# Joining projections side by side: matmuls of 512 columns in a two-layer decoder trunk

## The chip, the cores and the metric

One core of one Trainium2 chip. The metric is the time of one execution in device microseconds (us), as the median of several runs of the same kernel.

## The reference

A decoder trunk of two layers on 256 tokens and a model width of 1024, all in float32. Layer A is differential attention with a bias by distance, layer B is attention over a shared compressed latent; each is followed by a gated feed-forward with a short causal convolution and by a gated embedding. Only the projections in front of the two attentions matter here:

```python
# layer A: 8 heads, two maps of 64 each; x is (256, 1024), w_qkv is (1024, 3072)
qkv = rms_norm(x, attn_norm) @ w_qkv
q = rms_norm(qkv[:, :1024].reshape(256, 8, 2, 64), q_gain)        # a norm over each 64
k = rms_norm(qkv[:, 1024:2048].reshape(256, 8, 2, 64), k_gain)
v = qkv[:, 2048:].reshape(256, 8, 128)
# layer B: 16 heads; c_kv is (256, 256), c_q is (256, 512)
kv = (c_kv @ w_ukv).reshape(256, 16, 256)
k_nope, v = rms_norm(kv[..., :128], k_gain), kv[..., 128:]        # a norm over each 128
qq = (c_q @ w_uq).reshape(256, 16, 192)
q_nope = rms_norm(qq[..., :128], qn_gain)                          # a norm over each 128
q_pe = rotary(rms_norm(qq[..., 128:], qp_gain), pos)               # a norm over each 64
```

## The kernel before

Every float32 operand is held as two numbers of the type fp32r, a high part and a low part, and each product is made of three matmuls that add up in PSUM: high by high, high by low, low by high (`mm3`, L197). PE is TensorE, DVE VectorE, ACT ScalarE, POOL GpSimd, SP the engine that issues most DMAs.

**Weights.** The host cuts all weights into units of 128 x 1024 values (512 KB), in the order of their use (`_layout`, L1230). `load_unit` (L250) fetches the next unit into a ring of buffers and splits it: ACT casts the high part (`wh`, L246), and DVE or POOL subtracts it to get the low part (`wl`, L247). A share, 0.5 in layer A and 0.3 in most of layer B, says how many of these subtractions POOL takes. The ring has five buffers for fetched units and four pairs for split ones. SP issues the fetches in the order of the program, and a fetch whose buffer is not free holds all that follow it.

**Projections of layer A** (`proj_a`, L497). Four calls, each for two heads, and in each three blocks (`s` = 0, 1, 2): q, k and v, of 256 columns each. A block has eight k-tiles of 128 and two tiles of 128 tokens. The activations are the stationary operand of a matmul, the weights the moving one. `block` (L376) runs all k-tiles for the first token tile and then for the second one; both write halves of the same PSUM bank, which holds 512 values a partition. Two units, of four k-tiles each, feed a block. The first block of all (`first_block`, L675) takes its units as they come from DMA, in pieces of 256 KB with pieces of the activations between them; it splits both k by k on ACT and DVE (`get_first`, L663), 256 columns at a time, and uses a bank for each token tile.

**Norms** (`norm_block`, L337). ACT squares (L347 with a sum for blocks of 128, L350 for blocks of 64), DVE sums (L351) and adds epsilon (L353, L355), POOL takes the power -1/2 (L280), DVE multiplies out of PSUM (L361). A list of banks is squared and multiplied bank by bank. In layer A the epsilon carries the mean square of the token (`xs["eps"]`); it needs the statistics of the input, which `first_stats` (L688) loads and sums. Then `to_T` (L366) transposes by PE (L193) and splits the result (ACT L208, DVE L209); this is put off by `later`, for `LAG` = 6 us of the planner's own count of PE time.

**Order.** The builder's planner simulates the engines and sets from that, in advance, the order of instructions on each engine; on the chip each runs in that order. In the attention stages `weave` (L161) mixes two streams in the program: attention, and a filler (the projections still to come, the output projection). `bias_prep` (L399) makes the masks of the bias on DVE and 16 matmuls that sum them (L430); it is called from `proj_a` of the second head pair, and the planner puts its work into gaps from about 13 us on. The copies of its result (`bias_loads`, L451) are issued by SP after the fetches of units 10 to 12.

**Projections of layer B.** The order of the filler is `B_ORDER` (L63). An item ("kv", p) makes key and value for two heads: one unit with two k-tiles, each 256 key columns and 256 value columns; `kv_b` (L1090) runs a block for the key, its norm, and a block for the value into another bank. An item ("pe", c) makes the rotary parts of the queries of four heads (`pe_b`, L1110), an item ("qn", p) the other query parts of two heads (`qn_b`, L1129): a unit, a block and a norm each. Banks come from `bankF` (L1080): the first twelve by a list of the tags A, B and C, then always from tag A, which has three banks. The compressed query is ready after `cq_post`; an attention head needs its key, value and query, and its rotary part.

## Time and profile before

| | |
|---|---|
| three runs, median (lowest to highest) | 778.34 us (777.44 to 778.69) |
| the profiled execution | 777.55 us |
| its span, first to last instruction | 775.8 us |
| PE, DVE, ACT, POOL busy | 753.3, 570.8, 485.1, 272.7 us |
| mean granted clock of PE | 0.995 |
| read from memory | 125.75 MB |

The profile shows one execution. "Busy" is the time in which an engine has at least one instruction under way; matmuls overlap, so the mean duration of one is longer than the distance from one start to the next. A wait is idle time of an engine just before an instruction, with the one that ended it. The chain of work that ended last is followed back from the last instruction, each time to what released it. Times in rows count from the first instruction.

### The profile page before, as it was taken

To read this page: it belongs to the slowest core of one execution; us is meant where nothing else is said; L and a number is where in the kernel's file an instruction comes from. 1 tells how busy PE (TensorE), PEld (TensorE's weight loads), DVE (VectorE), ACT (ScalarE), POOL (GpSimd) and SP (SyncE) were. 2 spreads that over 40 slices of the span, in tenths; PEclk is the share of its full clock that TensorE was granted. 3 is DMA by queue.
4 is the path that set the end of the run, shared out by engine and by line. 5 is a ranking of instruction groups with operands and counts; after the bars stand their busy time and mean duration, and the time that the engine had idled before them with its cause. 6 is when DMAs were issued, how large, how long until landed. Compare 5 with 4: busy or idle time off the path is not lost.

```text
span 775.8 us, 16482 instructions
## 1 busy us (share of the span) xinstructions
PE 753.3 (97%) x6396; PEld 740.0 (95%) x6396; DVE 570.8 (74%) x1141; ACT 485.1 (63%) x1044; POOL 272.7 (35%) x187
## 2 busy tenths in 40 slices
PE   7999999999999999999898999999999999999996
PEld 6999989999999999999798999999999999999996
DVE  6677888568997796546788887876688778875545
ACT  6537876676566665447766876564676666655442
POOL 2655464232332511115616555221342332201231
PEclk9999999999999999999999999999999999999999
DMA  8994444256665576655354133344465566565531
GB/s 293 278 234 160 134 150 136 82 187 181 195 190 177 181 230 216 190 165 176 117 164 166 43 98 112 108 136 135 138 191 189 170 185 195 187 185 174 187 108 55
DMA packets 37519, 127.97 MB, mean 165 GB/s; under 512 B 4672, under 2 KB 6208, under 8 KB 37440
## 3 DMA queue, kind: packets, MB, share of 16 engines
q1 hardware_dynamic: 36432, 126.29, 52.5%
q8 instruction: 50, 0.82, 0.4%
q10 hardware_dynamic: 1008, 0.63, 0.3%
q14 instruction: 29, 0.24, 0.1%
HBM read 125.75 MB, written 1.15 MB: 164 GB/s over the span
## 4 chain that ended last, share of the span: by engine, by line
PE 82%; DVE 8%; ACT 4%; POOL 3%; issue 2%; DMA 1%; SPq 0%; POOLq 0%; ACTq 0%; DVEq 0%
PE pa L199 17%; PE pa L200 17%; PE pa L201 17%; PE pc L201 8%; PE pc L200 8%; PE pc L199 8%; DVE wl L247 2%; POOL wl L247 1%; DVE og L209 1%; ACT wh L246 1%; PE pt L193 1%; POOL s L280 1%; PE pb L482 1%; PE pb L549 1%; PE pc L193 1%
## 5 line engine op out<-in xcount | busy, mean ns | idle before, releaser
L246 ACT CAST wh<-st 128x1024 fp32r<-128x1024 f32 x221 | 230.8, 1049 | 166.5 <-issue 61.2
L247 DVE TENSOR_TENSOR wl<-st,wh 128x1024 fp32r<-128x1024 f32 x160 | 204.6, 1280 | 99.4 <-ACT wh L246 95.8
L247 POOL TENSOR_TENSOR wl<-st,wh 128x1024 fp32r<-128x1024 f32 x61 | 149.6, 2452 | 224.9 <-ACT wh L246 200.2
L201 PE MATMUL pa<-hgH,wl 128*128 128x256 f32 x496 | 140.7, 284 | 0.4 <-POOL wl L247 0.4
L199 PE MATMUL pa<-hgH,wh 128*128 128x256 f32 x496 | 140.4, 283 | 0.0
L200 PE MATMUL pa<-hgL,wh 128*128 128x256 f32 x496 | 140.3, 283 | 0.0
L200 PE MATMUL pa<-og,wh 128*128 128x256 f32 x352 | 99.8, 284 | 0.9 <-DVE og L209 0.9
L199 PE MATMUL pa<-og,wh 128*128 128x256 f32 x352 | 100.2, 288 | 0.1
L201 PE MATMUL pa<-og,wl 128*128 128x256 f32 x352 | 100.1, 285 | 0.0
L199 PE MATMUL pa<-wh,hgH 128*128 128x256 f32 x328 | 93.5, 289 | 4.8 <-DVE d L361 1.7
L304 POOL TENSOR_TENSOR ssq<-ssq,d 128x256 f32<-128x256 f32 x35 | 37.1, 1059 | 172.8 <-ACT d L303 172.4
L201 PE MATMUL pc<-hgH,wl 128*128 128x256 f32 x336 | 95.6, 285 | 1.0 <-DVE wl L247 1.0
L201 PEld LDWEIGHTS pa<-hgH,wl 128*128 128x128 f32 x496 | 95.2, 192 | 0.6 <-POOL wl L247 0.6
L200 PE MATMUL pc<-hgL,wh 128*128 128x256 f32 x336 | 95.1, 283 | 0.1
L199 PEld LDWEIGHTS pa<-hgH,wh 128*128 128x128 f32 x496 | 95.1, 192 | 0.1
L200 PEld LDWEIGHTS pa<-hgL,wh 128*128 128x128 f32 x496 | 95.1, 192 | 0.1
L199 PE MATMUL pc<-hgH,wh 128*128 128x256 f32 x336 | 95.0, 284 | 0.0
L200 PE MATMUL pa<-wl,hgH 128*128 128x256 f32 x328 | 93.4, 286 | 1.5 <-DVE wl L247 0.8
L201 PE MATMUL pa<-wh,hgL 128*128 128x256 f32 x328 | 93.1, 286 | 0.1
L200 PEld LDWEIGHTS pa<-og,wh 128*128 128x128 f32 x352 | 67.7, 192 | 1.1 <-DVE og L209 1.1
L199 PEld LDWEIGHTS pa<-wh,hgH 128*128 128x128 f32 x328 | 62.0, 191 | 6.9 <-DVE d L361 1.9
L199 PEld LDWEIGHTS pa<-og,wh 128*128 128x128 f32 x352 | 67.2, 192 | 0.8 <-ACT og L208 0.3
(304 smaller groups left out, 1913.6 us busy)
## 6 DMA issues: line engine op xcount, KB each, us to landing
st<-in_wall SPq DMA_DIRECT2D x225, 512.0 KB, 3.6
oh<-s SPq DMA_DIRECT2D x24, 128.0 KB, 6.6
hT<-in_x SPq DMA_DIRECT2D x4, 256.0 KB, 5.1
st<-in_wall SPq DMA_DIRECT2D x4, 256.0 KB, 5.3
st<-in_xn SPq DMA_DIRECT2D x2, 512.0 KB, 7.2
d<-in_p SPq DMA_DIRECT2D x2, 256.0 KB, 4.7
out_h<-hT SPq DMA_DIRECT2D x4, 128.0 KB, 1.9
out_h<-hT ACTq DMA_DIRECT2D x4, 128.0 KB, 1.9
```

Source lines behind the costliest of these rows:

```text
L193: lastmm[0] = T.transpose(o, i, ident).ins
L199: T.matmul(ps, lhsT=aH, rhs=bH, start=start, stop=False)
L200: T.matmul(ps, lhsT=aH, rhs=bL, start=False, stop=False)
L201: lastmm[0] = T.matmul(ps, lhsT=aL, rhs=bH, start=False, stop=stop).ins
L209: V.scalar_tensor_tensor(lo, src, scale, f(hi), ALU.mult, ALU.subtract)
L246: A.copy(hi, st)
L247: eng.tensor_sub(lo, st, f(hi))
L280: G.tensor_tensor(dst, src, neghalf[:, :n], ALU.pow)
L304: sqlast[0] = G.tensor_add(sq, sq, t).ins
L482: T.matmul(ps[:, i * 32:(i + 1) * 32], lhsT=lh, rhs=tb[z], start=z == 0, stop=z == 2)
L549: T.matmul(pss[e][:, a:b], lhsT=x[rows, j, t * P:(t + 1) * P], rhs=y[rows, j, :b - a], start=start, stop=stop)
```

## The change

Layer A: the host lays out q and k of a head pair side by side, two k-tiles of 512 columns to a unit, four units for both; v stays as it was. `proj_a` runs, for each token tile, all eight k-tiles with 512 moving columns into one bank (`wide`), and norms that bank (256 columns of q, 256 of k) as soon as it is there. The transposes of q and of k are both scheduled after the second tile's norm and take their sources from two tiles. The first block does q and k of the first pair in this way, from four units that come in halves. Layer B: `kv_b` does key and value in one pass of 512 columns, with a bank for each token tile; `pq_b` does four heads' rotary parts and two heads' other query parts in one pass; the remaining items ("qn", p) with odd p stay as they were. `B_ORDER` follows from that.

```diff
@@ -61,10 +61,10 @@
 def _b_order():
-    order = [("kv", 0), ("kv", 1), ("pe", 0), ("qn", 0), ("qn", 1), ("kv", 2), ("qn", 2), ("pe", 1)]
-    for p in range(3, 8):
-        order += [("kv", p)] + ([("pe", p // 2)] if p % 2 == 0 else []) + [("qn", p)]
-    order.insert(order.index(("qn", 6)) + 1, ("wo", (0, 4)))
+    order = [("kv", 0), ("kv", 1), ("pq", 0), ("qn", 1), ("kv", 2), ("pq", 1), ("kv", 3), ("qn", 3)]
+    for p in range(4, 8):
+        order += [("kv", p), ("qn", p) if p % 2 else ("pq", p // 2)]
+    order.insert(order.index(("pq", 3)) + 1, ("wo", (0, 4)))
     return order + [("wo", (4, 4)), ("wo", (8, 4))]
...
@@ -251,11 +250,10 @@
     first = []
-    for i in range(2):
-        pieces = fetch(2)
-        for k in (4 * i, 4 * i + 2):
-            nc.sync.dma_start(hT[:, k:k + 2], xT[:, k:k + 2])
-            st = next(pieces)
+    for i in range(4):
+        nc.sync.dma_start(hT[:, 2 * i:2 * i + 2], xT[:, 2 * i:2 * i + 2])
+        for st in fetch(2):
+            pass
         first.append(st)
...
@@ -384,6 +386,14 @@
                     k += 1
+
+    def wide(t, units, lH, lL, ps):
+
+        for i, u in enumerate(units):
+            for j in range(2):
+                k, c = 2 * i + j, slice(j * 512, (j + 1) * 512)
+                mm3(ps, lH[:, k, t * P:(t + 1) * P], lL[:, k, t * P:(t + 1) * P], u[0][:, c], u[1][:, c], k == 0,
+                    k == 2 * len(units) - 1)
...
@@ -495,41 +505,43 @@
     def proj_a(p):
-        todo = []
-
-        def post(s, ps):
-            dH, dL = qk(), qk()
-            if s < 2:
-                src = norm_block(ps, 4, 64, xs["eps"])
-                if p == 1:
-                    bst["after"] = bst.get("after", []) + nbv
-
-                def fin():
-                    to_T(src, dH, dL, gq[:, 0:1] if s == 0 else col(C_AK))
-                    QA[p]["qk"[s]] = dH, dL
-                later(LAG, fin)
-            else:
-                for t in range(NT):
-                    split(dH[:, t], dL[:, t], ps[:, t * S:(t + 1) * S], xs["r"][:, t:t + 1])
-                QA[p]["v"] = dH, dL
-
-        for s in range(3):
-            if p == 0 and s == 0:
-                ps = first_block()
-            else:
+        srcs = []
+
+        def norm_qk(t, ps):
+            srcs.append(norm_block(ps, 4, 64, xs["eps"][:, t]))
+            if p == 1:
+                bst["after"] = bst.get("after", []) + nbv
+
+        def fin(s, dH, dL):
+            to_T([x[:, s * S:(s + 1) * S] for x in srcs], dH, dL, gq[:, 0:1] if s == 0 else col(C_AK))
+            QA[p]["qk"[s]] = dH, dL
+
+        if p == 0:
+            pss = first_block()
+            yield 1
+            epsx()
+            first_stats()
+            for t in range(NT):
+                norm_qk(t, pss[t])
+        else:
+            us = [load_unit() for i in range(4)]
+            for t in range(NT):
                 ps = bankA()
-                us = [(load_unit(), 4) for i in range(2)]
-                block(8, us, S, 0, S, hgH, hgL, ps)
-            yield 1
-            todo.append((s, ps))
-            if p == 0 and s == 0:
-                epsx()
-            elif p == 0 and s == 1:
-                first_stats()
-            elif p == 1 and s == 0:
-                bias_prep()
-            while "r" in xs and todo:
-                post(*todo.pop(0))
+                wide(t, us, hgH, hgL, ps)
+                yield 1
+                if p == 1 and t == 0:
+                    bias_prep()
+                norm_qk(t, ps)
+        for s in range(2):
+            later(LAG, lambda s=s, pr=(qk(), qk()): fin(s, *pr))
+        us = [load_unit() for i in range(2)]
+        ps = bankA()
+        block(8, [(u, 4) for u in us], S, 0, S, hgH, hgL, ps)
+        yield 1
+        dH, dL = qk(), qk()
+        for t in range(NT):
+            split(dH[:, t], dL[:, t], ps[:, t * S:(t + 1) * S], xs["r"][:, t:t + 1])
+        QA[p]["v"] = dH, dL
...
@@ -662,10 +674,10 @@
-        for i in range(2):
+        for i in range(4):
             u = ring_pair()
-            for j in range(4):
-                k, q = 4 * i + j, slice(j * S, (j + 1) * S)
+            for j in range(2):
+                k, q = 2 * i + j, slice(j * 512, (j + 1) * 512)
                 A.activation(hgH[:, k], hT[:, k], AF.Copy, scale=col(C_ATTN[0] + k))
...
@@ -676,8 +688,8 @@
             for t in range(NT):
-                mm3(ps[t][:, :S], hgH[:, k, t * P:(t + 1) * P], hgL[:, k, t * P:(t + 1) * P],
-                    u[0][:, j * S:(j + 1) * S], u[1][:, j * S:(j + 1) * S], k == 0, k == NK - 1)
+                mm3(ps[t], hgH[:, k, t * P:(t + 1) * P], hgL[:, k, t * P:(t + 1) * P],
+                    u[0][:, j * 512:(j + 1) * 512], u[1][:, j * 512:(j + 1) * 512], k == 0, k == NK - 1)
         return ps
...
@@ -1091,15 +1102,14 @@
         u = load_unit()
-        ps = bankF()
-        block(2, [(u, 2)], 512, 0, S, ckH, ckL, ps)
-        yield 1.3
-        src = norm_block(ps, 2, P, EPS)
-        ps = bankF()
-        block(2, [(u, 2)], 512, S, S, ckH, ckL, ps)
-        yield 1.3
+        pss = [bankF() for t in range(NT)]
+        for t in range(NT):
+            wide(t, [u], ckH, ckL, pss[t])
+        yield 2.6
+        src = norm_block(pss, 2, P, EPS)
         kH, kL, vH, vL = qk(), qk(), qk(), qk()
-        split(vH.rearrange("p t x -> p (t x)"), vL.rearrange("p t x -> p (t x)"), ps)
+        for t in range(NT):
+            split(vH[:, t], vL[:, t], pss[t][:, S:])
...
@@ -1107,14 +1117,25 @@
-    def pe_b(c):
+    def q_fin(p, src):
+        qH, qL = qk(), qk()
+
+        def fin():
+            to_T(src, qH, qL, gq[:, 1:2])
+            QB[p]["q"] = qH, qL
+        later(LAG, fin)
+
+    def pq_b(c):
         while not cq_ready:
             yield None
-        u = load_unit()
-        ps = bankF()
-        block(4, [(u, 4)], S, 0, S, cqH, cqL, ps)
-        yield 2.6
-        qn = norm_block(ps, 4, 64, EPS)
+        us = [load_unit() for i in range(2)]
+        pss = []
+        for t in range(NT):
+            pss.append(bankF())
+            wide(t, us, cqH, cqL, pss[t])
+            yield 2.6
+        qn = norm_block(pss, 4, 64, EPS)
+        q_fin(2 * c, norm_block([x[:, S:] for x in pss], 2, P, EPS))
         qr = d_tile()
...
@@ -1266,8 +1281,9 @@
     for p in range(4):
-        for s in range(3):
-            natural(wqkv[:, s * 1024 + p * 256:s * 1024 + (p + 1) * 256], 4)
+        q, k, v = (wqkv[:, s * 1024 + p * 256:s * 1024 + (p + 1) * 256] for s in range(3))
+        natural(np.concatenate([q, k], axis=1), 2)
+        natural(v, 4)
     wo = f("a_w_o")[0]
...
@@ -1284,17 +1300,17 @@
-    def qpe(c):
-        natural(uq[:, 4 * c:4 * c + 4, P:].reshape(512, 256), 4)
-
     def qn(p):
-        natural(uq[:, 2 * p:2 * p + 2, :P].reshape(512, 256), 4)
+        return uq[:, 2 * p:2 * p + 2, :P].reshape(512, 256)
+
+    def pq(c):
+        natural(np.concatenate([uq[:, 4 * c:4 * c + 4, P:].reshape(512, 256), qn(2 * c)], axis=1), 2)
     for nm, a in B_ORDER:
         if nm == "wo":
             blocks(stationary(wo, range(a[0], a[0] + a[1])))
         else:
-            {"kv": kv, "pe": qpe, "qn": qn}[nm](a)
+            {"kv": kv, "pq": pq, "qn": lambda p: natural(qn(p), 4)}[nm](a)
     blocks(stationary(wo, range(12, 16)))
     ffn(1)
     wall = np.stack(units)

...
```

## Rows read from the trace of the kernel before

**Rows 1.** The page: busy time by engine, chain by engine.
```profile
PE 753.3 (97%) x6396; PEld 740.0 (95%) x6396; DVE 570.8 (74%) x1141; ACT 485.1 (63%) x1044; POOL 272.7 (35%) x187
...
PE 82%; DVE 8%; ACT 4%; POOL 3%; issue 2%; DMA 1%; SPq 0%; POOLq 0%; ACTq 0%; DVEq 0%
```

**Rows 2.** Timeline of PE: start, us, instruction, count, idle before, releaser.
```profile
5.74 0.50 PE L199 MATMUL pa<-wh,hgH 128*128 128x256 f32 x2 [0.97 <-ACT wh L671]
...
12.81 0.28 PE L201 MATMUL pa<-wh,hgL 128*128 128x256 f32 x1
...
14.77 0.83 PE L430 MATMUL pb<-ge,identb 128*128 128x384 bf16 x4
16.41 0.39 PE L200 MATMUL pa<-wl,hgH 128*128 128x256 f32 x1 [0.81 <-DVE wl L247]
...
19.33 0.38 PE L200 MATMUL pa<-wl,hgH 128*128 128x256 f32 x1 [0.57 <-POOL wl L247]
```

**Rows 3.** Windows: stretch, length, busy (count) by engine, clock, DMA share, GB/s.
```profile
4.00:13.00 9.00, 7.84 (x54) 6.72 (x54) 7.51 (x26) 6.22 (x17) 0.00 (x0) 1.00 1.00 368
26.00:50.00 24.00, 24.00 (x247) 23.99 (x245) 16.82 (x26) 10.46 (x15) 13.65 (x7) 1.00 1.03 238
600.00:620.00 20.00, 20.00 (x169) 20.00 (x168) 15.51 (x30) 12.36 (x22) 7.22 (x3) 1.00 0.55 178
```

**Rows 4.** Waits of PE in 395 to 530 us: us in total, times, longest.
```profile
PE pa L199 <- DVE d L361: 1.7, 1, 1.7
PE pa L199 <- DVE qk L206: 1.4, 1, 1.4
```

**Rows 5.** Timeline of PE: first and last of 23 projection matmuls of 256 columns.
```profile
23.11 0.28 PE L201 MATMUL pa<-wh,hgL 128*128 128x256 f32 x1
...
25.75 0.28 PE L199 MATMUL pa<-wh,hgH 128*128 128x256 f32 x1
```

**Rows 6.** Timeline of PE: four starts at 320 columns, 27 at 512.
```profile
381.18 0.31 PE L200 MATMUL pb<-wl,og 128*128 128x320 f32 x1
...
381.62 0.45 PE L201 MATMUL pb<-wh,og 128*128 128x320 f32 x2
...
385.80 0.40 PE L199 MATMUL pc<-wh,og 128*128 128x512 f32 x1
...
391.72 0.39 PE L201 MATMUL pc<-wh,og 128*128 128x512 f32 x1
```

**Rows 7.** Tile st, 0 to 30 us: count, ns min/median/max, starts.
```profile
L671 ACT CAST wh<-st x8: 388/402/407, 5.3 to 10.9; 128x256 fp32r<-128x256 f32 x8
L672 DVE TENSOR_TENSOR wl<-st,wh x8: 418/420/423, 5.8 to 11.7; 128x256 fp32r<-128x256 f32 x8
L246 ACT CAST wh<-st x7: 1040/1047/1058, 13.4 to 29.4; 128x1024 fp32r<-128x1024 f32 x7
L247 DVE TENSOR_TENSOR wl<-st,wh x3: 1220/1221/2053, 15.1 to 24.3; 128x1024 fp32r<-128x1024 f32 x3
L247 POOL TENSOR_TENSOR wl<-st,wh x3: 2405/2495/3766, 15.5 to 26.1; 128x1024 fp32r<-128x1024 f32 x3
```

**Rows 8.** Timeline of ACT: the activations' casts in the first block.
```profile
6.21 0.91 ACT L669 ACTIVATE hgH<-hT,cst 128x256 fp32r<-128x256 f32 x2 [0.21 <-DMA hT<-in_x]
```

**Rows 9.** Timelines of ACT and POOL: sixth unit's cast, first norm's power.
```profile
20.38 1.05 ACT L246 CAST wh<-st 128x1024 fp32r<-128x1024 f32 x1 [1.24 <-DMA st<-in_wall]
...
20.53 2.36 POOL L280 TENSOR_TENSOR s<-s,neghalf 128x8 f32<-128x8 f32 x1
```

**Rows 10.** Groups by shape, 395:530: count, busy us, mean ns, idle.
```profile
L361 DVE TENSOR_TENSOR d<-pa,s 128x512 f32<-128x512 f32 x18 | 12.3, 685 | 3.0 <-POOL s L280 2.9
L206 DVE TENSOR_TENSOR qk<-pa,qk 128x512 fp32r<-128x512 f32 x6 | 4.1, 683 | 0.0
...
L206 DVE TENSOR_TENSOR og<-pc,og 128x256 fp32r<-128x256 f32 x13 | 5.4, 414 | 0.2 <-ACT og L205 0.2
...
L280 POOL TENSOR_TENSOR s<-s,neghalf 128x4 f32<-128x4 f32 x16 | 17.9, 1117 | 34.4 <-DVE s L353 34.3
```

More of the change, by code (lines that the diff above doesn't have):

```diff
@@ L227, in fetch @@
         for j in range(pieces):
+            if j:
+                yield st
             lastfetch[0] = nc.sync.dma_start(st[:, j * n:(j + 1) * n], wall[u, :, j * n:(j + 1) * n]).ins
@@ L230, in fetch @@
                 hooks.pop(u)()
-            if pieces > 1:
-                yield st
-        if pieces == 1:
-            yield st
+        yield st
     def ring_pair(tag="w", bufs=BUF_W):
@@ L346, in norm_block @@
             for i in range(m):
-                A.activation(s2[:, i * P:(i + 1) * P], ps[:, i * P:(i + 1) * P], AF.Square, accum_out=ss[:, i:i + 1])
+                p, o = parts[i * len(parts) // m], (i % (m // len(parts))) * P
+                A.activation(s2[:, i * P:(i + 1) * P], p[:, o:o + P], AF.Square, accum_out=ss[:, i:i + 1])
         else:
@@ L366, in to_T @@
     def to_T(src, dH, dL, gcol, bank=None):
-        nb = src.shape[1] // (NT * P)
+        if not isinstance(src, list):
+            z = src.shape[1] // NT
+            src = [src[:, t * z:(t + 1) * z] for t in range(NT)]
+        nb = src[0].shape[1] // P
         pt = (bank or bankT)()
@@ L371, in to_T @@
             for j in range(nb):
-                i, o = t * nb + j, j * NT + t
-                transpose(pt[:, o * P:(o + 1) * P], src[:, i * P:(i + 1) * P])
+                o = j * NT + t
+                transpose(pt[:, o * P:(o + 1) * P], src[t][:, j * P:(j + 1) * P])
         split(dH.rearrange("p n x -> p (n x)"), dL.rearrange("p n x -> p (n x)"), pt[:, :NT * nb * P], gcol)
@@ L696, in first_stats @@
         rsqrt_(xs["r"], m, NT)
-        ep = cp.tile([P, 8], F32, name="epsx")
-        V.tensor_scalar(ep.rearrange("p (t n) -> p t n", t=NT), m.unsqueeze(2).to_broadcast([P, NT, 4]), EPS,
-                        None, ALU.mult)
+        ep = cp.tile([P, NT, 8], F32, name="epsx")
+        V.tensor_scalar(ep, m.unsqueeze(2).to_broadcast([P, NT, 8]), EPS, None, ALU.mult)
         xs["eps"] = ep
@@ L1135, in qn_b @@
         yield 2.6
-        src = norm_block(ps, 2, P, EPS)
-        qH, qL = qk(), qk()
-        def fin():
-            to_T(src, qH, qL, gq[:, 1:2])
-            QB[p]["q"] = qH, qL
-        later(LAG, fin)
+        q_fin(p, norm_block(ps, 2, P, EPS))
     oH, oL = [None] * 4, [None] * 4
@@ L1206, in attn_b @@
             yield 0.65
-    B_ITEMS = {"kv": kv_b, "pe": pe_b, "qn": qn_b, "wo": lambda a: wo(*a)}
+    B_ITEMS = {"kv": kv_b, "pq": pq_b, "qn": qn_b, "wo": lambda a: wo(*a)}
     def fl_b():
         for n, (nm, a) in enumerate(B_ORDER):
-            if n == 6:
+            if n == 5:
                 share[0] = SH_B
```

## The prediction, made before the changed kernel ran

> **What bounds the kernel now.** I read the page first: the busy table and the chain that ended last. PE is busy for 97% of the span and carries 82% of the chain; DVE, next, carries 8% [rows 1]. So matmul time is paid in full nearly everywhere, and work of the other engines is paid only where PE waits for it. Then I went to the two stages that the change touches, in order of time, and to the waits of PE alone. At the start PE runs its first projection matmul at 5.74 us and issues the last one of the query block at 12.81 us; the key block then stands twice, 0.81 us for a split on DVE and 0.57 us for one on POOL, and is in full flow only at 19.33 us [rows 2]. From 26 to 50 us PE is busy throughout and the DMA share is 1.03 [rows 3]: two resources are at their limit there. In layer B the two long waits of PE are 1.7 us for a norm's multiplication (L361) and 1.4 us for a value split (L206): both are readers of a PSUM bank that PE wants back [rows 4].
>
> **Joining the matmuls.** A weight block of 256 columns that met the same stationary tile as another becomes one of 512. Layer A: per pair of heads 2 token tiles x 8 k x 3 = 48 joined matmuls take the place of 96, four times: 192. Layer B: key and value 8 x 12 = 96, rotary and other queries 4 x 24 = 96. In all 384 fewer matmuls and weight loads, with the same columns. The price of a matmul is its distance to the next start. Projection matmuls of 256 columns start at 23.11 and, 22 steps later, at 25.75 us: 120 ns [rows 5]. In layer B's latent projections, 320 columns take 0.44 / 3 = 147 ns and 512 columns 5.92 / 26 = 228 ns [rows 6]. From 256 to 320 columns that is 0.42 ns a column, from 320 to 512 the same, so some 12.5 ns of each matmul do not depend on its columns. A joined pair gains 240 - 228 = 12 ns. The first 48 lie in the start, counted below; the other 336 give 336 x 12.3 = 4.1 us, on the path because PE is. Bounds: in a long even stretch 256 columns take 20 / 169 us = 118 ns [rows 3], which makes a pair worth 8.3 ns and the term 2.8 us; 4.4 us above.
>
> Here the Trainium skill would give another sum. "TensorE: Matmul & The Clock Gate", section "Wait — 56ns, not 53.3ns?", has a fixed cost of only about 2.5 ns on a matmul at the full clock; by it the term would be 336 x 2.5 ns = 0.8 us. The three widths of this trace disagree with it, with 12.5 ns [rows 5, 6], and I go by the trace.
>
> **The start.** Before, four k-tiles of q come with each unit; afterwards two of q and k side by side, so the first block needs all four first units and does both q and k. Its casts and subtractions keep going by k, now 512 wide. A cast of 256 takes 0.40 us and one of 1024 1.05 us, so 512 about 0.62; on DVE 0.42 and 1.22, so about 0.69 [rows 7]. With the cast of the activations (0.91 us for two [rows 8]) ACT needs 1.07 us a k, DVE about as much. Data: twelve pieces of 256 KB; at 368 GB/s [rows 3] one piece takes 0.71 us, a k needs a piece of weights and half a piece of activations, 1.07 us. PE needs 6 x 0.228 = 1.37 us a k: it is now the slowest, 8 x 1.37 = 10.9 us. It starts at 5.74 plus 0.2 (wider cast), loses about 0.5 to the first subtraction and ends near 17.4 us. The 16 bias matmuls that now fill the gaps (four take 0.83 us with the last one's tail, 0.17 each [rows 2], 2.7 us) come on top: 20.1 us. Before, 14 of the key's 48 matmuls have run by 19.33 us, by the count of such rows; 34 (4.1 us) and four of the bias ones (0.7) are left: 24.1 us. So PE is some 4 us ahead here, mainly because the key's units no longer go through whole-unit splits, of which one was 3.77 us on POOL [rows 7].
>
> Not all of that lasts. The value block needs units five and six. The sixth landed at 20.38 us, held by its issue [rows 9]; afterwards its buffer is free sooner, and by the volume it lands near 19.2. Cast to 20.3, then POOL: 2.4 us [rows 7], so 22.7; or 25.1 if the norm's power of 2.36 us goes first, as it does now [rows 9]. With the 36 matmuls behind it (4.3 us) the value block ends at 27.0 to 29.4 us, against 24.1 + 48 x 0.12 = 29.9. That is 0.5 to 2.9 ahead; I take the middle, 1.7. Bounds: 4.0 if POOL never holds it; -1.4 if both tiles' powers go ahead of the subtraction. What is late next is the DMA queue at share 1.03, which can eat this gain, not more. SP's queue is passed too: constants and positions now stand behind four more pieces of weights, 1.0 MB or 2.8 us later, and the masks for the bias behind them; cover is the first block, which itself lasts 4.6 us longer.
>
> In the other three head pairs of layer A one token tile's pass now wants four units in 5.5 us, where a pass over two wanted two in 5.8; the ring holds four split pairs. The fourth gets its pair when the value block before it is done, and needs 1.05 + 2.4 = 3.45 us [rows 7]; PE reaches it after 18 x 0.228 = 4.1. The cover is 0.65 us, gone when a power of 2.36 us stands ahead on POOL: then 1.7 us late. I take -0.5 in all (in two of three, attention's matmuls can go in between); bounds 0 and -5.1. The norms themselves are as many and as wide as before, one for each token tile instead of one for q and one for k. Layer A together: +1.2.
>
> **Layer B.** Norms and splits that read one bank of 512 now read two of 256: one multiplication and one value split more for each key-value item, two multiplications more for each query item. On DVE two of 0.414 replace one of about 0.684, +0.145 us [rows 10]: 24 of them, 3.5 us, with 1 to 2 us on ACT. Both have idle time there and the sum hides it, except where PE waits for a bank. That is the real cost. A key bank used to be normed while the value's matmuls ran, and the value bank was free after one split; now both banks wait for both token tiles and for the norm, whose power alone is 1.12 us [rows 10]. With three "A" banks, a query item fills two, and the second bank of the item behind it must wait until both its norms have read them. Such a wait was 1.4 and 1.7 us [rows 4]. Against it: the planner puts attention matmuls there, and the first head gets its q together with its rotary part. I take -1.5 us; bounds +3.1 (both present waits go) and -12 (twelve joined items, a wait of about 1 us each).
>
> **Sum.** 4.1 + 1.2 - 1.5 = 3.8 us off. The profiled execution took 777.55 us (span 775.8 and 1.75 around it), which gives 773.75; the median of the runs, 778.34, is 0.8 above that execution, so the forecast is 774.5 us.
>
> **Rivals.**
> 1. Slower: the banks. In layer B every joined item, eight and four, holds both banks until its norm is read, and PE waits about 1 us for each. For: both long waits of this stage are of that kind [rows 4]. Against: they are only two among some twenty items, and PE has attention to run. It decides once the banks are held longer than the matmuls that come before the next claim: behind a query item 6 x 0.228 = 1.4 us of the next item's first tile, and the attention in between. Time: -12 in place of -1.5, 785.0 us.
> 2. The ring: the fourth unit is late each time, 3 x 1.7 = 5.1 us in place of 0.5. For: POOL's 2.4 us and a cover of 0.65. Against: PE did not stand there before [rows 3]. 774.5 + 4.6 = 779.1 us, no change.
> 3. The joined matmuls save hardly anything: the surplus of a matmul stays with its columns instead of vanishing with the instruction. Against: 320 and 512 columns [rows 6]. With 0.8 in place of 4.1: 777.8 us, no change. This is also what the skill's rule above would make of it.
> 4. Better: the start keeps its 4.0, and the two bank waits go because the first q and rotary part come sooner: 774.5 - 2.3 - 4.6 = 767.6 us.
>
> **How the numbers follow.** Forecast 0.50, its own range 771 to 777; rival 1 0.17, rival 2 0.13, rival 3 0.05, rival 4 0.15. The range of 768 to 781 leaves out most of rival 1, and half of rival 4. About 0.2% (1.6 us) is what can be told from no change. Faster: most of the forecast and rival 4, 0.61. Same: rivals 2 and 3 and the forecast's upper end, 0.20. Slower: rival 1 and a little of 2, 0.19.
>
> **What would show it.** The step between two projection matmuls of 512 columns: 226 to 230 ns, and 384 matmuls fewer on the page. The value block of the first head pair done at 27 to 29.5 us, no 3.77 us subtraction on POOL before it. Waits of PE in layer B: a sum near 5 us confirms the forecast, 10 or more with L361, L206 or L209 named is rival 1; waits for wl (L247) on POOL in the second to fourth head pairs are rival 2. The prediction is wrong if PE's own total does not fall by 3 us or more, or if the gain at 30 us is lost to the DMA by 60 us.

## The result: 796.3 us, slower by 2.3%

| | before | after |
|---|---|---|
| median (lowest to highest), 4 runs each | 778.41 us (777.44 to 778.69) | 796.26 us (794.23 to 797.94) |
| the profiled execution, its span | 777.55, 775.8 us | 797.94, 796.2 us |
| mean granted clock of PE | 0.995 | 0.979 |
| first scores of layer A | 65.4 us | 62.0 us |
| token mean behind layer A's attention | 161.1 us | 168.9 us |
| token mean ahead of layer B | 384.7 us | 392.5 us |
| token mean behind layer B's attention | 562.6 us | 583.5 us |

The ratio is 1.023, with an interval of 1.020 to 1.0261. The stage times come from two lines of the source: the first matmul of a head's scores (L549 before, L561 after), and the matmuls that average over a token (L309 before, L307 after). The changed kernel was 3.4 us ahead at the first scores, 7.8 behind at the end of layer A's attention, no further behind ahead of layer B, and lost 13.1 more in layer B's attention. Everything else kept its length. The three stage ends in PE's timeline before:

```profile
161.08 0.39 PE L309 MATMUL pt<-ones,ssq 128*128 128x2 f32 x3
...
384.66 0.39 PE L309 MATMUL pt<-ones,ssq 128*128 128x2 f32 x3
...
562.58 0.39 PE L309 MATMUL pt<-ones,ssq 128*128 128x2 f32 x3
```

and after:

```profile
168.95 0.39 PE L307 MATMUL pt<-ones,ssq 128*128 128x2 f32 x3
...
392.54 0.39 PE L307 MATMUL pt<-ones,ssq 128*128 128x2 f32 x3
...
583.50 0.39 PE L307 MATMUL pt<-ones,ssq 128*128 128x2 f32 x3
```

The page of the kernel after, busy time and chain by engine; they answer to [rows 1]:

```profile
PE 765.1 (96%) x6012; PEld 731.0 (92%) x6012; DVE 573.3 (72%) x1163; ACT 487.9 (61%) x1053; POOL 270.1 (34%) x186
...
PE 80%; DVE 9%; ACT 5%; DMA 3%; issue 2%; POOL 1%; SPq 0%; POOLq 0%; ACTq 0%; DVEq 0%
```

384 matmuls are gone, and yet PE is busy 11.8 us longer: it was slower, not more loaded. The timeline of PE after, at the end of the first block and of the first pair's value block (columns as in [rows 2]):

```profile
17.08 0.39 PE L201 MATMUL pa<-wh,hgL 128*128 128x512 f32 x1
17.31 1.01 PE L440 MATMUL pb<-ge,identb 128*128 128x384 bf16 x5
...
28.25 0.28 PE L201 MATMUL pa<-wh,hgL 128*128 128x256 f32 x1
28.38 0.40 PE L199 MATMUL pa<-wh,hgH 128*128 128x512 f32 x1
28.61 0.40 PE L200 MATMUL pa<-wl,hgH 128*128 128x512 f32 x1
28.84 0.39 PE L201 MATMUL pa<-wh,hgL 128*128 128x512 f32 x1
29.07 0.40 PE L199 MATMUL pa<-wh,hgH 128*128 128x512 f32 x1
```

The first block ends at 17.5 us, the value block at 28.5, and the steps of 512 columns are 0.23 us. Up to here the forecast held. Then the waits of PE after, from 405 to 550 us, which answer to [rows 4]:

```profile
PE pb L199 <- ACT qk L208: 4.5, 1, 4.5
PE pt L193 <- DVE d L360: 1.7, 1, 1.7
PE pa L199 <- DVE hT L647: 1.3, 2, 0.8
PE pa L199 <- DVE qk L206: 1.0, 1, 1.0
PE pc L193 <- DVE ex L1186: 0.8, 1, 0.8
PE pa L201 <- DVE hgL L206: 0.8, 1, 0.8
```

With three smaller ones these are 11.2 us. Before, the waits of this stage added up to 4.7 us, the two of [rows 4] and four of 0.3 to 0.6; the longest one now is new. Only 1.2 of the 11.2 us are a key, value or query projection waiting for its bank (`pa` behind L206, 1.0, and L360, 0.2); the two longest waits are for operands. Last, windows of the kernel after: the columns are the stretch, its length, busy time of PE, PEld, DVE, ACT and POOL, the granted clock, DMA share and GB/s.

```profile
110.90:117.70 6.80, 6.80 (x35) 6.58 (x34) 4.83 (x8) 4.27 (x11) 6.63 (x4) 0.50 0.63 203
134.80:141.60 6.80, 6.66 (x32) 6.36 (x31) 3.79 (x9) 2.68 (x8) 1.39 (x2) 0.50 0.18 72
431.70:441.90 10.20, 7.05 (x20) 5.68 (x21) 6.41 (x13) 3.42 (x13) 8.04 (x8) 0.50 0.49 156
472.70:479.50 6.80, 6.80 (x35) 6.80 (x34) 4.22 (x18) 3.09 (x16) 5.43 (x9) 0.50 0.00 0
```

The same view of the kernel before has one such stretch in its attention stages:

```profile
113.40:116.80 3.40, 3.40 (x19) 3.40 (x18) 1.87 (x11) 2.98 (x10) 1.92 (x2) 0.50 0.74 293
```

The clock was at 0.50, the lower of its two levels (1.2 GHz), for 30.6 us after and 3.4 before. Ahead of the first three stretches PE had stood, 1.3 us at 109, 1.6 at 132 and 4.5 at 429, and the third began while it still stood; ahead of the fourth no wait is listed. Taking the distance from each matmul's start to the next, less that of its shape at the full clock, and adding up, the excess is 53.3 us after and 28.2 before. Of this 14.1 and 1.5 lie in the half-clock stretches. So of 25.1 us more, 12.6 lie in half-clock stretches, and in 3.3 of these PE stands. Less the 4.7 us that the joined matmuls save by their steps, the 25.1 are the 20.4 us between the two spans; as the excess is counted with the same steps, this sum is no test of the saving.

### The profile page after: what moved, and what is told of

Its sections match the earlier page's. It is cut to its first block, busy times and chain, and to the rows that moved or that the text cites. A ratio compares the mean times of both kernels' runs of the same rounds, so it can differ in the third digit from the quotient of the medians.

```text
span 796.2 us, 15717 instructions
## 1 busy us (share of the span) xinstructions
PE 765.1 (96%) x6012; PEld 731.0 (92%) x6012; DVE 573.3 (72%) x1163; ACT 487.9 (61%) x1053; POOL 270.1 (34%) x186
## 4 chain that ended last, share of the span: by engine, by line
PE 80%; DVE 9%; ACT 5%; DMA 3%; issue 2%; POOL 1%; SPq 0%; POOLq 0%; ACTq 0%; DVEq 0%
PE pa L199 17%; PE pa L200 16%; PE pa L201 16%; PE pc L201 8%; PE pc L200 8%; PE pc L199 8%; DMA oh<-s 2%; DVE wl L246 2%; ACT wh L245 2%; PE pt L193 1%; PE pb L561 1%; DVE og L209 1%; PE pc L193 1%; PE pb L199 1%; PE pb L200 1%
## 5 line engine op out<-in xcount | busy, mean ns | idle before, releaser
L245 ACT CAST wh<-st 128x1024 fp32r<-128x1024 f32 x219 | 228.1, 1049 | 151.6 <-issue 61.6
L246 DVE TENSOR_TENSOR wl<-st,wh 128x1024 fp32r<-128x1024 f32 x159 | 200.0, 1259 | 89.2 <-ACT wh L245 79.8
L246 POOL TENSOR_TENSOR wl<-st,wh 128x1024 fp32r<-128x1024 f32 x60 | 145.8, 2429 | 211.0 <-ACT wh L245 181.3
L199 PE MATMUL pa<-og,wh 128*128 128x256 f32 x352 | 101.6, 291 | 1.3 <-DVE hT L647 1.3
L200 PE MATMUL pa<-og,wh 128*128 128x256 f32 x352 | 101.4, 288 | 0.0
L199 PE MATMUL pa<-wh,hgH 128*128 128x512 f32 (+1 forms) x208 | 73.3, 360 | 2.1 <-DVE qk L206 1.0
L200 PE MATMUL pa<-wl,hgH 128*128 128x512 f32 (+1 forms) x208 | 74.2, 357 | 0.9 <-DVE wl L246 0.8
L201 PE MATMUL pa<-wh,hgL 128*128 128x512 f32 (+1 forms) x208 | 73.5, 353 | 0.8 <-DVE hgL L206 0.8
L278 POOL TENSOR_TENSOR s<-s,neghalf 128x4 f32<-128x4 f32 (+2 forms) x30 | 44.7, 1491 | 76.3 <-DVE s L352 45.5
L199 PEld LDWEIGHTS pa<-og,wh 128*128 128x128 f32 x352 | 68.4, 196 | 2.1 <-DVE hT L647 1.9
L200 PEld LDWEIGHTS pa<-og,wh 128*128 128x128 f32 x352 | 68.9, 196 | 0.4 <-DVE og L209 0.2
```

What stands on the lines that cost most here:

```text
L199: T.matmul(ps, lhsT=aH, rhs=bH, start=start, stop=False)
L200: T.matmul(ps, lhsT=aH, rhs=bL, start=False, stop=False)
L201: lastmm[0] = T.matmul(ps, lhsT=aL, rhs=bH, start=False, stop=stop).ins
L245: A.copy(hi, st)
L246: eng.tensor_sub(lo, st, f(hi))
L278: G.tensor_tensor(dst, src, neghalf[:, :n], ALU.pow)
```

## The experiments

All times are medians of several runs, and the ratio with its 95% interval is against runs of the kernel before on the same chip (777.7 to 778.4 us).

### Which layer

Each layer's part of the change alone, with the other layer as before.

```diff
 # layer A alone, against the changed kernel
-    B_ITEMS = {"kv": kv_b, "pq": pq_b, "qn": qn_b, "wo": lambda a: wo(*a)}
+    B_ITEMS = {"kv": kv_b, "pe": pe_b, "qn": qn_b, "wo": lambda a: wo(*a)}
 # layer B alone
-            us = [load_unit() for i in range(4)]
+                us = [(load_unit(), 4) for i in range(2)]
```

> Layer A as in the changed kernel, layer B as before. In the trace of the changed kernel layer A's attention ends 7.8 us later than before (first token mean at 168.9 against 161.1 us), layer B loses 13 us more. Theory 1 (readers of a shared bank take turns, and what is read late arrives late at the first head): in layer A a joined bank has one norm only, so its part here is small; the loss must then come from q and k arriving together late. Theory 2 (four units wanted in one pass, ring of four pairs): the loss sits here, in the second to fourth head pairs. Either way 784 to 788 us; about 775 us, as I had forecast for layer A, would mean that A's loss in the changed kernel comes only with layer B's part of the change (a plan made anew as a whole).

Measured 785.28 us, ratio 1.0098 (1.0083 to 1.0114).

> Layer A as before, layer B as in the changed kernel. Theory 1: the loss of layer B is its own, 790 to 793 us, and the first exponential of layer B comes about 57 us after the token mean in front of it, against 46 before. If layer B suffers only from what layer A left behind: 778 us or less.

Measured 788.91 us, ratio 1.014 (1.0125 to 1.0156). The two add up: 0.98 and 1.40% against 2.3% together. There are two losses, one in each layer, each beside its own saving of matmuls (192 x 12.3 ns = 2.4 us).

### Parts of a layer

Only the first block joined in layer A; and in layer B only key with value.

```diff
 # first block alone, against layer A alone
-            us = [load_unit() for i in range(4)]
-            for t in range(NT):
+            for s in range(2):
+                us = [(load_unit(), 4) for i in range(2)]
                 ps = bankA()
-                wide(t, us, hgH, hgL, ps)
+                block(8, us, S, 0, S, hgH, hgL, ps)
...
```

> Only the first block of all is joined (q and k of the first head pair, four units in halves); the other three head pairs and layer B as before. The changed kernel reaches layer A's first head 3.4 us earlier than before; if that is kept, 775 us. If the DMA queue or attention behind it eats the gain, 778 us. A loss here would put layer A's trouble into the first block.

Measured 777.95 us, ratio 1.0003 (0.9987 to 1.0019). It is ahead by 1.8 us at the first scores (63.6) and by 0.9 at the token mean (160.2), and the end shows nothing. So layer A's loss, 7.3 us, is all in the second to fourth pairs.

> Only key and value of layer B are joined; rotary parts and other queries keep their own items and their order, layer A as before. Theory 1: a joined key-value bank has one norm and one split, so it loses little: 777 to 781 us, and most of layer B's 13 us belongs to the joined query items with two norms in one pair of banks. A loss by longer holding of banks alone would be shared by eight items here and four there: 785 us or more.

Measured 781.80 us, ratio 1.0049 (1.0034 to 1.0064). One row of its PE timeline is as long as the whole loss:

```profile
425.72 0.77 PE L199 MATMUL pa<-wh,hgH 128*128 128x512 f32 x1 [4.33 <-DVE qk L206]
```

PE stands for a value split (L206) that wants nothing but its matmuls, and these had been done for long. In program order it came behind the key's norm. ACT's cast of the value waited for DVE's multiplication of the key out of the same bank (L362), and this for POOL's power, here in the timelines of ACT, POOL and DVE:

```profile
424.74 0.70 ACT L205 CAST qk<-pa 128x256 fp32r<-128x256 f32 x2 [1.83 <-DVE d L362]
...
422.40 1.85 POOL L280 TENSOR_TENSOR s<-s,neghalf 128x4 f32<-128x4 f32 x1 [0.17 <-DVE s L354]
...
421.13 1.13 DVE L354 TENSOR_SCALAR s<-s 128x4 f32<-128x4 f32 x1
```

The power waited in turn for DVE's small step ahead of it (L354). That step took 1.13 us, where others of its shape took 0.16, and it ended 0.03 us after a weight subtraction on POOL (419.86 to 422.23); why it was held is not shown.

### Layer B: hold the banks less, or change the order of their readers

The kernel after has the same pattern, here in ACT's timeline; in brackets the idle time ahead of an instruction and what ended it:

```profile
413.33 0.37 ACT L205 CAST qk<-pa 128x256 fp32r<-128x256 f32 x1 [0.70 <-DVE d L360]
...
422.84 0.28 ACT L346 ACTIVATE d<-pa 128x128 f32<-128x128 f32 x1 [2.64 <-DVE d L360]
```

The first is the value's cast behind the key's multiplication. In the second the squares of the other query part (L346) wait for the rotary part's multiplication (L360): two engines that only read, different columns, but of one bank. PE pays:

```profile
425.86 0.77 PE L193 MATMUL pt<-ident,d 128*128 128x128 f32 x4 [1.65 <-DVE d L360]
...
433.85 0.47 PE L199 MATMUL pb<-qk 128*128 128x128 f32 x1 [4.46 <-ACT qk L208]
...
435.96 0.77 PE L199 MATMUL pa<-wh,hgH 128*128 128x512 f32 x1 [1.00 <-DVE qk L206]
```

The long one, 4.46 us, is for the split of a query (L208) whose transposes had ended at 426.6 us. ACT came to it at 433.10, in program order behind weight casts and behind another value cast that waited for the key's multiplication:

```profile
432.50 0.70 ACT L205 CAST qk<-pa 128x256 fp32r<-128x256 f32 x2 [0.26 <-DVE d L360]
433.10 0.69 ACT L208 ACTIVATE qk<-pt,gq 128x512 fp32r<-128x512 f32 x1
```

Two edits of layer B alone, each against its 788.91 us. One copies the banks to SBUF first, so that the norm holds none:

```diff
         for t in range(NT):
+            A.copy(kd[:, t * S:(t + 1) * S], pss[t][:, :S])
             split(vH[:, t], vL[:, t], pss[t][:, S:])
+        src = norm_block(kd, 2, P, EPS)
...
+        for t in range(NT):
+            x = d_tile()
+            A.copy(x, pss[t])
+            pss[t] = x
```

> Layer B joined as in the changed kernel, layer A as before; but each joined bank is emptied at once: ACT copies a query bank whole (512 columns, about 0.59 us), and of a key-value bank the key's half, beside the value's split; the norms then read the copies. Some 10 us more of ACT in all. Theory 1 (a joined bank is held until every reader had its turn, behind a power on POOL, and PE stands for it): most of the 11 us of layer B comes back, 777 to 781 us against 788.9. Theory 3 (order of the items and the plan as such): no change, 787 to 791 us, or worse by the copies.

Measured 783.68 us, ratio 1.0066 (1.0042 to 1.0091): 5.2 of 11 us come back, for 0.8 us of copies on ACT for each key-value item and 1.2 us for each query item. It takes the norm off the bank, so the turns of the readers go together with the holding, and it cannot tell the two apart. The other edit adds no instruction and moves only the readers (the planner makes a new plan for it, as for every edit here): all squares of an item first, then the value split, and the multiplications last.

```diff
-        src = norm_block(pss, 2, P, EPS)
+        end = norm_sq(pss, 2, P, EPS)
         for t in range(NT):
             split(vH[:, t], vL[:, t], pss[t][:, S:])
+        src = end()
...
-        qn = norm_block(pss, 4, 64, EPS)
-        q_fin(2 * c, norm_block([x[:, S:] for x in pss], 2, P, EPS))
+        ends = norm_sq(pss, 4, 64, EPS), norm_sq([x[:, S:] for x in pss], 2, P, EPS)
+        qn = ends[0]()
+        q_fin(2 * c, ends[1]())
```

> Layer B joined, layer A as before; only the order of the readers of a joined bank differs: all squares first (rotary and other part), and the value's split ahead of the key's multiplication. No copies; a bank is still held until its norm is multiplied out. If the loss of layer B lies in the readers' turns: 778 to 782 us. If it lies in how long a bank is held: 786 to 789 us.

Measured 781.37 us, ratio 1.004 (1.0026 to 1.0053): order alone gives back 7.5 of 11 us, more than the copies. The bank is still held until its norm is multiplied out, though with the turns gone it comes free sooner too. The first exponential of layer B comes 45.4 us after the token mean, as before (46), where after took 57. What is left shows in the same place. PE's timeline of this kernel has three waits there:

```profile
418.98 0.33 PE L199 MATMUL pb<-qk 128*128 128x128 f32 x1 [1.10 <-ACT qk L208]
...
424.13 0.33 PE L199 MATMUL pb<-hgH,peH 128*128 128x128 f32 x1 [1.05 <-ACT peH L205]
...
426.32 0.48 PE L201 MATMUL pb<-hgH,peL 128*128 128x128 f32 x1 [1.08 <-DVE peL L206]
```

and a window that begins within the third of them (columns as above) stands at the half clock:

```profile
425.80:432.60 6.80, 6.28 (x29) 6.28 (x30) 4.48 (x19) 4.46 (x18) 5.43 (x10) 0.50 0.25 86
```

The waits are for the first head's operands; 6.8 us at the half clock cost at most 3.4. Layer B still loses 3.2 us; that these are the same was not tried.

### Layer A: one bank for transposes?

With layer A joined the third pair's transposes take 17 us from first to last (73.1 to 90.1 us), with only the first block joined 11 (70.2 to 81.1). The row of the transpose tile in 69 to 92 us (least, median and longest duration in ns, first and last start), with layer A joined:

```profile
L193 PE MATMUL pt<-ident,d x8: 270/272/329, 73.1 to 90.1; 128*128 128x128 f32 x8
```

and with the first block alone:

```profile
L193 PE MATMUL pt<-ident,d x8: 272/272/330, 70.2 to 81.1; 128*128 128x128 f32 x8
```

The fifth head's scores follow. PE's timeline with layer A joined:

```profile
95.82 0.95 PE L561 MATMUL pb<-qk 64*128 64x128 f32 x12
```

and in the other kernel:

```profile
87.35 0.95 PE L568 MATMUL pb<-qk 64*128 64x128 f32 x12
```

First attempt: k's transposes through another tag's banks; then that together with the copies of layer B in the changed kernel.

```diff
-            to_T(..., gq[:, 0:1] if s == 0 else col(C_AK))
+            to_T(..., gq[:, 0:1] if s == 0 else col(C_AK), bankC if s else None)
```

> Layer A joined as in the changed kernel, layer B as before; but the transposes of k go through a bank of tag C instead of the single bank of tag T. In the run with layer A alone q's first two transposes of the third head pair took bank T at 73 us, q's last two came at 82 us when the second token tile was normed, and k's only at 90 us; the fifth head started at 95.8 us, against 87.3 with separate q and k. Theory 1a (the one transposing bank, held by q from the first tile's norm to the second's): the fifth head some 5 to 7 us earlier, 778 to 781 us against 785.3. Theory 2 (four units at once, ring of four pairs): no change, 784 to 787 us.

Measured 788.10 us, ratio 1.0137 (1.0103 to 1.0171), if anything slower than layer A alone.

> The whole change, with both remedies: banks emptied at once in layer B, k's transposes through a bank of tag C in layer A. If theories 1 and 1a name the whole loss, what is left is the shorter matmuls: 774 to 778 us. If the loss lies elsewhere: 790 us or more.

Measured 794.93 us, ratio 1.022 (1.0193 to 1.0246), not clearly better than the changed kernel; the 5.2 us that the copies gave in layer B and the 2.8 that the second bank cost in layer A would make 793.9. A second bank is not the cure. In the first of the two runs the fifth head came 3 us sooner (92.6), but the time did not; that k now shares its bank's turns with attention may be why, and is not shown.

Second attempt: transpose by token tile. A tile's q and k go through the one bank together as soon as that tile is normed.

```diff
+            later(LAG, lambda: fin(t, src))
+
+        def fin(t, src):
+            pt = bankT()
+            for j in range(4):
+                transpose(pt[:, j * P:(j + 1) * P], src[:, j * P:(j + 1) * P])
+            for s in range(2):
...
+                split(*(x[:, :, t * P:(t + 1) * P] for x in dst[s]),
+                      pt[:, s * S:(s + 1) * S].rearrange("p (n x) -> p n x", x=P),
+                      gq[:, 0:1] if s == 0 else col(C_AK))
```

> Layer A joined, layer B as before, but transposed by token tile: as soon as a tile's bank is normed, its two q and two k blocks go through the transpose bank together, instead of q of both tiles and then k of both tiles after the second tile's norm. It adds two splits of 256 columns in place of one of 512 (about 0.15 us each, off PE). Theory (q and k come late together because both wait for the second tile's norm and then take turns in the single transpose bank): with layer A joined the third pair's last transposes came at 90.1 us against 81.1 us with only the first block joined, and its first scores at 95.8 against 87.3; here the last transposes should come near 82 and the scores by 89, the time falls from 785.3 to 779 to 781. Rival (the second tile's norm itself is the late thing: 7.1 us from its last matmul at 70.7 to its multiplication at 77.8, behind POOL's subtraction and a full DVE): scores still past 92, time 784 to 786.

Measured 783.04 us, ratio 1.0072 (1.0051 to 1.0093), a third of the 7.3 us, between the two expectations. The last transposes came at 83.2, as wanted, but the scores only at 92.2. Its timelines show why in part. DVE:

```profile
85.77 0.47 DVE L209 SCALAR_TENSOR_TENSOR qk<-pt,gq,qk 128x256 fp32r<-128x256 f32 x1
...
87.58 0.48 DVE L209 SCALAR_TENSOR_TENSOR qk<-pt,cst,qk 128x256 fp32r<-128x256 f32 x1
```

and ACT:

```profile
86.27 0.48 ACT L208 ACTIVATE qk<-pt,cst 128x256 fp32r<-128x256 f32 x1
```

k's cast (86.27) starts 0.03 us after q's subtraction has ended (85.77 + 0.47): turns again, this time in the transpose bank. So, both casts first:

```diff
+            for s in range(2):
+                A.activation(hl[s][0], ps[s], AF.Copy, scale=gc[s])
+            for s in range(2):
+                V.scalar_tensor_tensor(hl[s][1], ps[s], gc[s], f(hl[s][0]), ALU.mult, ALU.subtract)
```

> Transposing by token tile again, with the order of the readers of the transpose bank changed: both casts on ACT first, then both subtractions on DVE. In the run by tile (783.0 us) the third pair's last transposes came at 83.2 us as the theory wanted, but k's cast on ACT began only when q's subtraction on DVE was done (86.27 behind 86.23, and in the same way 62.66 behind 62.62), its own subtraction ended at 88.06, and the fifth head's scores came at 92.2 instead of 87.3. Theory (the other half of layer A's loss is again two engines taking turns in one bank): scores by 90, time 780 to 781.5. Rival (the second tile's norm and the full DVE in this stretch hold the pair, whatever the order of the readers): scores at 92 or later, 782.5 to 784.

Measured 782.32 us, ratio 1.0057 (1.0041 to 1.0072), just under the rival's range and above the theory's. k's split ended at 85.4 instead of 88.1, but the scores came at 91.3: they stand in PE's order behind the next pair's tile (81.5 to 90.0). So the readers' order in this bank is not the rest of the loss.

### Layer A: scores side by side

PE's sequence, matmul by matmul, shows something more. A head's scores are two maps, each on 64 rows of the array. The timeline of PE before, at one head's scores:

```profile
70.90 0.96 PE L549 MATMUL pb<-qk 64*128 64x128 f32 x12
```

and after, at another's:

```profile
66.56 0.95 PE L561 MATMUL pb<-qk 64*128 64x128 f32 x6
67.44 0.50 PE L201 MATMUL pa<-wh,hgL 128*128 128x512 f32 x1
...
68.33 0.95 PE L561 MATMUL pb<-qk 64*128 64x128 f32 x6
```

Twelve matmuls, the maps in turn, take 0.96 us; six of one map alone take 0.95. Side by side the second map is free. The distances add up to 8.86 us for all eight heads before, 12.07 with layer A joined and 12.19 after, 3.3 us of PE time that is on no list of waits. The order written for PE had put projection matmuls between the maps. Here the Trainium skill agrees: "TensorE: Matmul & The Clock Gate", "Part 3: Packing small matmuls — row/col tiling", has matmuls of few rows run at once on different row groups of the array; by it too an order that separates the maps gives this up. The edit holds the other ten behind the first of each map, with layer A alone, with tiles and casts, and as a control in the kernel before:

```diff
+                        with contextlib.ExitStack() as held:
+                            for i in mm[:2] if len(mm) > 1 else []:
+                                held.enter_context(tc.issue_after(i))
-                        T.matmul(pss[e][:, a:b], ...)
+                            mm.append(T.matmul(pss[e][:, a:b], ...).ins)
```

> Layer A joined and layer B as before (785.3 us so far), with one thing more: after the first matmul of each of a head's two maps, the other ten of the scores are issued only behind both, so that the maps' matmuls, each on 64 rows of the array, stay side by side. Twelve in one group take 0.88 us, two groups of six 0.88 us each; with layer A joined nearly every head came in two groups (12.07 us for the scores' matmuls of all eight heads), in the kernel before mostly in one (8.86 us). Theory (the two maps' banks come free at different moments and the order written for PE puts projection matmuls in between, so the halves no longer overlap: 3.2 us of layer A's 7.4 us): scores' matmuls back to about 9.3 us in all, time 782 to 783. Rival (the halves only fill time in which PE would stand for the second bank): their sum falls but PE waits as much more, 784.5 to 786.

Measured 783.65 us, ratio 1.0064 (1.0044 to 1.0084), against 785.28, between its two expectations. The scores fell to 8.57 us, 3.5 less, and 1.6 of it arrived. Part of the rest is a wait that is new in PE's timeline (lines stand one further in this kernel):

```profile
109.95 0.90 PE L194 MATMUL pc<-ident,ex 128*128 128x128 f32 x3 [2.63 <-DVE og L210]
```

> Transposing by tile with casts first (782.3 us, scores' matmuls 11.70 us in all), and the two maps' matmuls kept together as well. If the halves are the rest of layer A's loss, about 2.4 us come off: 779 to 780.5, and the gap to the first block alone (778.0) is closed. Rival (as above, waits take their place): 781.5 to 783.

Measured 784.01 us, ratio 1.0072 (1.0049 to 1.0095). It tells little. The scores took 11.56 us. The planned order still put others between the ten, and the last two heads came for the most part in a stretch at the half clock, the longest of any trace here (columns as above):

```profile
111.60:128.70 17.10, 17.09 (x86) 15.57 (x85) 12.23 (x42) 11.69 (x41) 5.18 (x4) 0.50 0.32 111
```

Their 24 matmuls cost 3.9 us there and would have cost about 2.0 at the full clock, an estimate from groups of the same size in layer A with the hold alone.

> Control: the kernel before with the same hold on the two maps. There only the first head is in two groups (0.88 us to gain) and the planned order splits three others once more, so the theory expects 777 to 778.5, no change; if the hold itself cost or gave several us, the other two runs could not be read.

Measured 780.91 us, ratio 1.0031 (1.0017 to 1.0045), against the expectation: the hold itself costs 2.8 us where nearly nothing was apart. Its scores took 9.6 us in place of 8.86; what the rest is, is not shown. So the other two mix a gain and a price, and what the halves are worth alone is not settled by them.

### Both layers repaired, and the best of the parts

> The changed kernel with both orders repaired: transposes by token tile in layer A, all squares first and the value split ahead of the norm's multiplication in layer B. The two layers' losses added up so far (7.4 and 11.1 of 18.4). With layer B at +3.0 (the run of that order alone was 781.4) the sum gives 781 to 784 us if transposing by tile repairs layer A, and 788 us if it does not. Faster than 778 only if the saving of the joined matmuls (4.1 us by 336 x 12.3 ns) shows at last; nothing so far says so.

The changed kernel by tile in layer A and with the readers' order in layer B: 784.31 us, ratio 1.0095 (1.0071 to 1.012), 12 of 18 us back, and the parts' sum (0.72 and 0.40%) within the interval.

> The changed kernel with all three orders: by tile with casts first in layer A, squares and value split first in layer B. By the sum of the parts, 784.3 less what the casts' order gives: 781 to 783 by the theory, 784 to 785 by the rival. If all of the loss came from order, the 384 matmuls saved (4.7 us by 12.3 ns each) would bring it to 774; the parts say it will not get there.

With casts first as well: 787.03 us, ratio 1.0103 (1.0066 to 1.0141), no better than without.

> Only the two joins that looked least harmful: the first block of layer A (778.0 alone, no change) and key with value in layer B (781.8 alone), with the value split and the squares ahead of the key's multiplication. Theory (turns in the bank were all of the loss of key and value, 4.0 us): the 4.33 us stand of PE at 421 us goes, and 96 matmuls fewer give 96 x 12.3 ns = 1.2 us: 776.5 to 778, the only version that could be below before. Rival (two banks held by one item cost something whatever the order): 779.5 to 781.

The first block, and key with value in the readers' order: 779.15 us, ratio 1.002 (1.0002 to 1.0038). Order removed most of this item's loss, not all. No combination was below the kernel before.

## Why the prediction was wrong, point by point

3.8 us off were forecast, and 17.9 more were measured; PE's busy time, which was to fall by 3 us or more, rose by 11.8. Two terms of the sum failed, the other pairs of layer A and layer B, and a third, the start, came to nothing.

**Joined matmuls: right by the steps.** Steps of 228 to 230 ns and 384 matmuls fewer: 384 x 12.3 ns = 4.7 us. No run shows this saving as time; the first block alone saved 48 matmuls and took as long as before. With the 2.5 ns of the Trainium skill ("TensorE: Matmul & The Clock Gate", "Wait — 56ns, not 53.3ns?") an estimate of it would be 1.0 us; the three widths decide against it.

**The start: right at 30 us, and worth nothing in the sum.** The sum took 1.7 us off for it. Measured: 17.5 us for the first block (17.4 forecast), 28.5 for the value block (27.0 to 29.4), 3.4 us at the first scores (1.7). But the run with only this block joined is at 1.0003: most of what is early at 62 us has gone by 160. It was forecast that the DMA queue could eat it, and the chain after does run through DMAs from 33.6 to 49.7 us; that this is what ate it was not tried.

**The other three pairs of layer A, -0.5 us: failed.** Measured 785.28 - 777.95 = 7.3 us lost, 9.1 with the 1.8 us that 144 joined matmuls saved, beyond the bound of -5.1. The step asked whether the weights would be in time, and that was the wrong question: with layer A joined PE waits for no wl between 60 and 110 us, so rival 2 has no support either. Instead, what the step called "as many and as wide as before", the norms, had changed in kind: a bank normed for q alone completes q; a bank normed for one token tile completes nothing. q and k of a pair were both done only after the second tile, their transposes crowded, heads five and seven came 8.5 and 6.7 us late (95.8 against 87.3, 117.4 against 110.7), and the scores' maps fell apart. That this is the loss is shown in part only. Transposing by tile gave back 2.2 us, casts first 0.7 more (not beyond the runs' scatter), keeping the maps together 1.6; but all three in one kernel gave 784.0 us, 1.3 less than none. More than half of the loss stays without a shown cause. A rival that no run tests is the plan: every edit gets a new order on all engines, and two edits that were meant to cost nothing or to gain (the hold in the kernel before, the second bank for k) cost 2.8 us each, so a part of this size may be the plan's own.

**Layer B, -1.5 us: failed, and it is the larger one.** Measured 788.91, 11 us lost, 13 with the 2.4 saved. The place and the size were rival 1's (12 us), which had a chance of 0.17 because "only two among some twenty items" waited before. Its mark is met only by the sum: the waits are 11.2 us, but those that name its lines (L361, here L360; L206; L209) make 4.3 of them, and a projection waited for its bank for 1.2. What the step counted wrong are the readers: before, a bank had one norm or one split to read it; joined, it has a norm's squares on ACT, its multiplication on DVE, and a split or a second norm beside it. The added instructions were priced at their durations, and their place in the order at nothing. Order alone was 7.5 of the 11 us. Rival 1's own reason, banks held too long, is not shown: copying them out at once took away holding and turns together and brought less, 5.2.

A rule of the Trainium skill speaks of this, and the prediction did not weigh it. "PSUM — Partial Sum Buffer", section "PSUM bank collisions raise a hardware error ⚠️", says that two engines on the same 32 partitions of one bank must be kept apart even if both only read, and that a compiler puts a dependency between them. The waits of ACT for DVE here (2.64 us at 422.84) agree with it.

**The clock: not in the sum at all.** 12.6 of the 25 us of excess lie at the half clock, the 3.3 us of standing included. These are not the price of the clock alone, which is probably smaller: of the changed kernel's executions one spanned 796.2 us at a mean clock of 0.979 and one 792.4 at 0.991, 3.8 us for some 19 us less at the half clock. Over the 172 executions of the experiments, each against the others of its kernel, a us at the half clock went with 0.34 us of time (an estimate from the mean clocks). No row of before suggested the clock (0.995), but a forecast that adds waits to PE in a stage where it is the bound may have to price them at more than their length.

**Rivals 3 and 4** are out: the steps are as short as forecast, the start's gain did not last, and the waits for banks did not all go.

## What to carry to other kernels

Before two results are joined in one PSUM bank, list its readers by engine and program order: each later one inherits the wait of the one ahead, so put the readers that wait for nothing first, and a norm's multiplication last. Ask of a joined tile which operand is complete when it is done; a cheaper matmul that delivers every operand last can cost the stage behind it more. A saving of 12 ns a matmul is 5 us in 384, and one wait for another engine's turn (4.3 us) is nearly the same.

## What the runs showed that was not expected

- Matmuls of 64 rows on different halves of the array, issued in turn, take 0.96 us for twelve and 0.95 for six of one half.
- Around waits of PE of 1.3 to 4.5 us, and once without one, the granted clock was 0.50 for 6.8 to 10.2 us at a time, 30.6 us in the execution after. With the readers' order mended one such stretch of 6.8 us was left in layer B, which began in the third of three waits of 1.1 us each; before, the two waits of 1.7 and 1.4 us [rows 4] had none behind them.
